# A one-layer diffusion block on one core: x first, modulation weights in larger groups, other feed order, five gate tiles in the scans

## The chip, the core and the metric

The kernel runs on one core of a Trainium2 chip. The metric is the device time of one execution in microseconds (us). A core has TensorE (PE in the profile; PEld is its weight load), VectorE (DVE), ScalarE (ACT), GpSimd (POOL), and SyncE (SP), which here issues all transfers. Each engine works through its own instructions in order. Which engine gets an instruction, and in what order, is settled when the program is built.

## The reference

One adaLN-modulated layer with two parallel head groups, cut to what matters here:

```python
mod = silu(c) @ w_ada + b_ada;  shift, scale, gate = split(mod, 3)     # w_ada: 2048 x 6144
h  = rms_norm(x, norm_w) * (1 + scale) + shift                         # x: 512 x 2048, latent tokens
hc = rms_norm(ctx, norm_w) * (1 + scale_c) + shift_c                   # ctx: 256 x 2048, with c_ctx
qkv_g, z_g, gates, q_a, k_a, v_a, z_a = split(h @ w_in)                # the same for hc
# group A, 8 heads of 128: q, k, v = silu(conv5(qkv_g)); chunked gated delta rule in 64-token chunks,
# forward and backward, context first, then latent; o = rms_norm(o_f + o_b) * silu(z_g)
# group B, 8 query heads on 2 kv heads: rms-normed q and k, rotary; softmax(q k / sqrt(128)) v * silu(z_a)
y = concat(A, B) @ w_out;   out = rms_norm(x + gate * y, final_norm_w)
```

All of it is float32. A product that needs full precision on fast matmuls is made of three: each operand is split into a rounded part (`hi`) and the rest (`lo`), and hi·hi, hi·lo and lo·hi are summed.

## The kernel before, in words

All projections are tiles of 128 output columns, accumulated over 16 K tiles (`KT`, 128 rows of the 2048 each), with three matmuls per K tile for the 512 latent tokens and, where it is needed, three for the 256 context tokens. A weight piece is four K tiles: a transfer, a cast to `hi` on ACT (L137), a subtraction that gives `lo` (L138; on DVE for the first 14 pieces, then on POOL).

**First stage.** Six blocks of 128 tokens (two of ctx, four of x) are loaded; ACT sums their squares (L284), POOL takes the power -0.5 (L224), DVE multiplies the block by 1/rms (L289), PE transposes it in 128x128 pieces (L295), and DVE and ACT copy the result to SBUF (L302, L300). For each group of K tiles (`GROUPS`, ten groups of one or two) `ada` reads the scale and shift columns of w_ada (32 MB in all, L315), multiplies them by the two conditioning vectors (L319) and turns the result into columns (L327). `make_h` forms h for a K tile on DVE (hf, L365), its hi on ACT (L367) and its lo on DVE (L373). `project` (L383, L385) then adds that K tile to five projections at once: k, q and v of head 0, k and q of head 1; the 32 gate columns (L388) follow at the end of each K tile. While a K tile is projected, `ada` of the group after the next one is slipped in between.

**From the first stage to the scans.** The five accumulators go to SBUF through `conv` (L199, L202: ACT copies from PSUM; L210 to L218: the convolution, its taps on DVE at L214). Gates, then `gdn_prep(0)`, prepare head 0. Meanwhile `feeding()`, a generator of projection matmuls, is drawn upon by `pull(n)` for n moving columns at a time: it is what PE does between the steps of other work.

**Scans.** For each head h, `gdn_scan` has 12 steps; each is a chain PE, DVE (rh, L818), PE (L827), ACT (L831, L834), PE (L838), DVE (state, L844). A step draws F1 + F2 + F3 = 9800 columns from the feeds, and `gdn_prep(h + 1)` runs in between. Before scan h starts, the loop pulls until v of head h + 1 has been fed. The feeds in order: v of head 1, the four tiles of attention's k and v, then for each head k, q, v and a tile of attention's q, and at the end `NZA` = 3 tiles of the attention gate z_a (`zal`), kept in DRAM.

**Attention.** 16 units (8 heads, two halves of 256 queries) and one for the last values. PE's order is written out by hand, and that of ACT, DVE and POOL too: transposed probabilities (L1218), scores (L154 to L156, `s`), `fill(FS)`, one more transpose, `fill(FV)`, values (`o`), `fill(FQ)`, on odd units the next head's q, `fill(FR)`. `fill(1)` is one K tile of the gate projections not made yet (`zl`, L1281: three matmuls of 512 columns): 13 tiles of 16 such fills, 12 fills a unit. Then the output projection (`po`) and the final norm.

## Time and profile before

Three runs took 1424.14, 1420.56 and 1421.66 us: the median is 1421.66 us. The profiled execution took 1418.51 us, its span on the core is 1416.3 us.

| engine | busy us | share of the span |
|---|---|---|
| PE | 1281.7 | 90% |
| PEld | 1021.2 | 72% |
| DVE | 767.8 | 54% |
| ACT | 614.5 | 43% |
| POOL | 517.3 | 37% |

In the views that follow, a row of a timeline has the start in us, the length in us, the engine, line, operation, output<-input with its shape, and in brackets how long the engine had been idle and what ended that. A row of the table by stage has for each engine its busy time and count of instructions, then the TensorE clock that was granted as a share of full speed (PEclk), the transfers' share of the 16 DMA engines, and GB/s. A wait is told as its total, the number of times, and the longest.

### The profile page before, as it was taken

How to read it: one execution, taken by the hardware profiler on the slowest of the kernel's cores; microseconds unless marked ns; L12 is line 12 of the kernel's file. 1: busy time of each engine (PE TensorE's matmuls, PEld its weight loads, DVE VectorE, ACT ScalarE, POOL GpSimd, SP SyncE). 2: the span in 40 equal slices, each digit the busy share in tenths (PEclk: the TensorE clock that was granted, in tenths of full speed). 3: DMA queues.
4: the chain of work that ended last, by engine and by line, in shares of the span. 5: the costliest groups of instructions: out<-in, count | busy, mean ns of one | idle time of the engine just before them, and what ended most of it. 6: DMA issues, size and time to landing. Idle time of an engine off the chain costs nothing.

```text
span 1416.3 us, 24550 instructions
## 1 busy us (share of the span) xinstructions
PE 1281.7 (90%) x9214; PEld 1021.2 (72%) x9214; DVE 767.8 (54%) x1666; ACT 614.5 (43%) x1531; POOL 517.3 (37%) x465
## 2 busy tenths in 40 slices
PE   4789979999999999999999999769989899999997
PEld 3345667888877877778777777547777778777785
DVE  5435487255565665656476643436666675544322
ACT  5212253334545445454444534445666663433221
POOL 1111300234434444343443534324877672011320
PEclk8999999999999999999999999879999999999999
DMA  8999412332232323223232344323555442474312
GB/s 263 328 346 290 120 53 59 93 67 66 78 66 59 72 69 75 62 57 84 58 77 61 81 90 121 96 86 113 150 148 161 129 112 60 163 236 143 92 37 95
DMA packets 234617, 163.49 MB, mean 115 GB/s; under 512 B 62146, under 2 KB 206619, under 8 KB 233475
## 3 DMA queue, kind: packets, MB, share of 16 engines
q1 hardware_dynamic: 234499, 161.93, 40.6%
q8 instruction: 72, 1.18, 0.4%
q14 instruction: 46, 0.38, 0.1%
HBM read 148.33 MB, written 13.56 MB: 114 GB/s over the span
## 4 chain that ended last, share of the span: by engine, by line
PE 52%; DVE 19%; issue 9%; ACT 7%; DMA 6%; POOL 5%; SPq 1%; POOLq 0%; DVEq 0%; ACTq 0%
PE vl L172 5%; PE zl L1281 4%; PE kl L172 3%; PE vx L174 3%; DVE cacc_v L214 3%; PE kvl L172 3%; DMA wada<-in_w_ada 2%; DVE cacc_k L214 2%; PE po L155 2%; PE tsh L838 2%; PE po L156 2%; PE po L154 2%; DVE rh L818 2%; DVE tmh L694 2%; PE ql L172 2%
## 5 line engine op out<-in xcount | busy, mean ns | idle before, releaser
L230 POOL TENSOR_TENSOR sdh<-sth,egl 128x256 f32<-128x256 f32 x80 | 55.7, 696 | 176.5 <-DVE sth L844 70.6
L1323 POOL TENSOR_TENSOR gacc<-graw,gacc 128x512 f32<-128x512 f32 x60 | 89.9, 1498 | 48.9 <-ACT graw L1321 38.8
L138 POOL TENSOR_TENSOR wlo_z<-wraw_z,whi_z 128x512 fp32r<-128x512 f32 x52 | 70.6, 1360 | 55.9 <-ACT whi_z L137 55.9
L823 ACT ACTIVATE oqh<-ksh,egsw 64x128 f32<-64x128 f32 x128 | 46.4, 362 | 100.4 <-DVE rh L818 99.5
L818 DVE SCALAR_TENSOR_TENSOR rh<-ksh,negeg,vtokh 64x128 f32<-64x128 f32 x176 | 61.1, 347 | 47.3 <-PE ksh L806 44.3
L1281 PE MATMUL zl<-hhL,whi_z 128*128 128x512 f32 x208 | 85.4, 411 | 0.0
L1281 PE MATMUL zl<-hL,whi_z 128*128 128x512 f32 x208 | 82.4, 396 | 0.0
L1281 PE MATMUL zl<-hhL,wlo_z 128*128 128x512 f32 x208 | 82.3, 395 | 0.0
L844 DVE TENSOR_TENSOR sth<-sdh,tsh 128x256 f32<-128x256 f32 x80 | 33.7, 421 | 89.5 <-PE tsh L838 84.3
L155 PE MATMUL po<-wlo_wo,mh 128*128 128x512 f32 x192 | 76.7, 399 | 3.8 <-DVE wlo_wo L138 3.8
L154 PE MATMUL po<-whi_wo,mh 128*128 128x512 f32 x192 | 76.0, 398 | 2.5 <-ACT whi_wo L137 1.5
L156 PE MATMUL po<-whi_wo,ml 128*128 128x512 f32 x192 | 76.0, 396 | 0.0
L138 DVE TENSOR_TENSOR wlo_wo<-wraw_wo,whi_wo 128x512 fp32r<-128x512 f32 x48 | 37.7, 794 | 64.7 <-ACT whi_wo L137 64.5
L838 PE MATMUL tsh<-vsh,ktok 128*128 128x128 f32 x352 | 58.0, 289 | 10.1 <-ACT vsh L831 5.3
L353 POOL TENSOR_TENSOR w0l<-w0r,w0h 128x640 fp32r<-128x640 f32 x16 | 24.9, 1561 | 107.4 <-PE cctx L388 56.4
L903 DVE TENSOR_TENSOR ptl<-pt,pth 128x512 fp32r<-128x512 f32 x48 | 31.9, 688 | 58.4 <-ACT pth L902 58.1
L1429 POOL TENSOR_TENSOR yx<-yx,tt 128x512 f32<-128x512 f32 x12 | 17.1, 1441 | 127.0 <-DVE tt L230 67.9
L838 PEld LDWEIGHTS tsh<-vsh,ktok 128*128 128x128 f32 x352 | 49.0, 196 | 18.7 <-ACT vnh L834 8.8
L214 DVE SCALAR_TENSOR_TENSOR cacc_v<-craw,cvT,cacc_v 128x256 f32<-128x256 f32 (+1 forms) x64 | 41.6, 696 | 33.9 <-ACT cacc_v L210 33.5
L827 PE MATMUL tsh<-rh,UU 128*128 128x128 f32 x176 | 38.4, 301 | 21.8 <-DVE rh L818 21.7
L137 ACT CAST whi_wo<-wraw_wo 128x512 fp32r<-128x512 f32 x48 | 29.3, 618 | 59.5 <-PE po L156 42.6
L827 PEld LDWEIGHTS tsh<-rh,UU 128*128 128x128 f32 x176 | 28.4, 194 | 33.7 <-issue 15.2
(492 smaller groups left out, 4155.4 us busy)
## 6 DMA issues: line engine op xcount, KB each, us to landing
wada<-in_w_ada SPq DMA_DIRECT2D x64, 512.0 KB, 8.0
graw<-in_w_ada SPq DMA_DIRECT2D x64, 256.0 KB, 2.7
wraw_z<-in_w_in SPq DMA_DIRECT2D x52, 256.0 KB, 3.0
wraw_wo<-in_w_out SPq DMA_DIRECT2D x48, 256.0 KB, 3.0
wraw_v<-in_w_in SPq DMA_DIRECT2D x28, 256.0 KB, 2.8
wraw_k<-in_w_in SPq DMA_DIRECT2D x24, 256.0 KB, 2.8
wraw_q<-in_w_in SPq DMA_DIRECT2D x24, 256.0 KB, 3.0
xs<-in_x SPq DMA_DIRECT2D x4, 1024.0 KB, 4.8
```

The lines of the kernel that those rows point to most:

```text
L138: (lo_eng or G).tensor_tensor(out=lo, in0=raw, in1=hi, op=ALU.subtract)
L154: T.matmul(out, lhsT=lh, rhs=rh, start=start, stop=False, skip_group_check=True)
L155: T.matmul(out, lhsT=lh, rhs=rl, start=False, stop=False, skip_group_check=True)
L156: T.matmul(out, lhsT=ll, rhs=rh, start=False, stop=stop, skip_group_check=True)
L172: T.matmul(pl, lhsT=lw, rhs=rt[0], start=st, stop=sp, skip_group_check=True)
L214: V.scalar_tensor_tensor(out=x, in0=raw[:, i0 + j:i0 + j + m], scalar=w(j), in1=x, op0=ALU.mult, op1=ALU.add)
L230: eng.tensor_tensor(out=out, in0=x, in1=y, op=ALU.mult)
L818: V.scalar_tensor_tensor(out=r[rows], in0=ks[rows, d], scalar=gsc["negeg"][rows, gcol:gcol + 1], in1=vtok[rows, p], op0=ALU.mult, op1=ALU.add)
L827: T.matmul(ts[:, 2], lhsT=UU[:, w], rhs=r, start=True, stop=True, skip_group_check=True)
L838: T.matmul(ts[:, d], lhsT=ktok[:, p, half], rhs=vs, start=True, stop=True, skip_group_check=True)
L1281: T.matmul(pl, lhsT=lw, rhs=rt, start=k == 0 and m == 0, stop=k == KT - 1 and m == 2, skip_group_check=True)
L1323: G.tensor_tensor(out=acc, in0=raw, in1=acc, op=ALU.add)
```

## The change

- **x first.** The transfers of x and ctx are issued ahead of the six small ones, and seven buffers of 1 MB instead of five (`BIG`) serve x and w_ada. DVE no longer multiplies a block of x: it makes a 128x128 diagonal matrix `rd` of 1/rms, and PE multiplies the block by it with an ordinary float32 matmul where there was a transpose. Six of eight copies out are DVE's.
- **Groups.** `GROUPS` = (2, 4, 4, 4, 2). `ada` handles shift and scale one after the other, with 1 MB transfers whose rows are 1 KB (two K tiles) or 2 KB (four). The gate columns become `gate_sums`, which stand right behind `make_h` of a pair of K tiles and ahead of that group's projections. Weights of K tile k + 2 are asked for when K tile k starts.
- **Accumulators.** `take` copies all five out of PSUM at once, ahead of the convolutions, two of them into new buffers (`xraw`). In the first piece of a feed with context tokens, the latent matmuls all come first.
- **Feeds.** New order; all `lo` pieces of feeds are POOL's. `NZA` is 5: two gate projections (2 x 48 matmuls of 512 columns) go from attention's fills to the feeds. FV is 3 (was 4), FR 2 (was 3): 10 fills a unit.

```diff
-FS, FV, FQ, FR = 4, 4, 1, 3
+FS, FV, FQ, FR = 4, 3, 1, 2
-NZA = 3
+NZA = 5
-    GROUPS = (1, 1, 2, 2, 2, 2, 2, 2, 1, 1)
+    GROUPS = (2, 4, 4, 4, 2)
...
-        if lo_eng is None and cnt[0] <= 14:
-            lo_eng = V
...
+            if pc is not None and kq == 0:
+                for out, m, n_ in ((pl, 0, SEQ), (pc, 1, CTX)):
+                    for x in passes:
+                        one(out, m, *x)
+                        yield n_
+                continue
...
+    def take(pl, pc, raw=None):
+        raw = next_craw() if raw is None else raw
         if pc is not None:
             S.copy(raw[:, 2:2 + CTX], pc)
+        S.copy(raw[:, CTX + 4:CTX + 4 + SEQ], pl)
+        return raw
...
-    BIG = 5
+    BIG = 7
...
-        V.tensor_scalar(out=xt_, in0=xt_, scalar1=ssx[:, t:t + 1], scalar2=None, op0=ALU.mult)
+        rd = p0.tile([128, 128], F32, tag="rd", bufs=2, name=f"rd{t}")
+        V.tensor_scalar(out=rd, in0=ident, scalar1=ssx[:, t:t + 1], scalar2=None, op0=ALU.mult)
...
+                T.matmul(tp[:, i], lhsT=xt_[:, c0:c0 + 128], rhs=rd, start=True, stop=True, skip_group_check=True)
...
-                T.transpose(out=tp[:, i], in_=xt_[:, c0:c0 + 128], identity=ident)
...
+        cols, rows = n * 128, 16 // n
+        for s in range(2):
+            ada_ps = gtile([128, 512], f"ada{g}_{s}")[:, :cols]
+            for j in range(KT // rows):
+                wt = big([128, rows, cols], f"wada{g}_{s}_{j}")
...
+    def gate_sums(p_):
+        for k in (2 * p_, 2 * p_ + 1):
+            for j in range(3):
+                T.matmul(gps[32 * j:32 * j + 32], lhsT=wg[:, k], rhs=hfs[k][:, 256 * j:256 * j + 256],
+                         start=False, stop=k == KT - 1, skip_group_check=True)
...
+    def ahead():
+        gate_sums(0)
+        yield
+        for g in range(1, len(GROUPS)):
+            yield from ada(g)
+            for p_ in make_h(g):
+                yield
+                gate_sums(p_)
+            made.add(g)
+            yield
...
+    todo = ahead()
     for g in range(len(GROUPS)):
+        while g not in made:
+            next(todo)
+        for k in range(first_k[g], first_k[g] + GROUPS[g]):
+            if k + 2 < KT:
+                first_weights(k + 2)
+            for i, _ in enumerate(project(k)):
+                if k or i >= 2:
+                    next(todo, None)
...
+    raws = [take(klat, cctx[:, 0]), take(qlat, None), take(vlat, cctx[:, 1]),
+            take(klat1, cctx1[:, 0], xraw[0]), take(qlat1, None, xraw[1])]
...
     def feeding():
+        yield from feed_kva(0)
+        yield from feed_qa(0)
+        yield from feed_kva(1)
         yield from feed_v(1)
-        for i in range(4):
-            yield from feed_kva(i)
-        fed.add("kva")
         for h in range(2, NH):
             yield from feed_k(h)
             yield from feed_q(h)
             yield from feed_v(h)
-            yield from feed_qa(h - 2)
-        for h in range(6, NH):
+            if h in (3, 5):
+                yield from feed_qa(1) if h == 3 else feed_kva(2)
+        yield from feed_kva(3)
+        fed.add("kva")
+        for h in range(2, NH):
             yield from feed_qa(h)
         for h in range(NZA):
             yield from feed_za(h)
```

**PE in the first stage, where a group's h is ready.** Names end in a buffer number; hf2 is h of K tile 2, klat0 the k of head 0, cctx1 holds the gate sums. Before, the gates of K tile 2 follow its projections:

```order
L319 MATMUL ada4_737<-wada4_2_764,cs_113 32x512 x4
L383 MATMUL qlat0_514<-hhL_70,w0h2_604 128x512
L383 MATMUL qlat0_514<-hL2_627,w0h2_604 128x512
L383 MATMUL qlat0_514<-hhL_70,w0l2_605 128x512
L319 MATMUL ada4_737<-wada4_3_774,cs_113 32x512 x4
L383 MATMUL qlat1_516<-hhL_70,w0h2_604 128x512
L383 MATMUL qlat1_516<-hL2_627,w0h2_604 128x512
L383 MATMUL qlat1_516<-hhL_70,w0l2_605 128x512
L388 MATMUL cctx1_518<-hf2_617,wg_428 32x256 x3
L383 MATMUL klat0_512<-hhL_70,w0h3_611 128x512
```

Now the second half of a group's modulation, then the gates of its four K tiles, and only then K tile 2's first projection:

```order
L333 MATMUL ada1_1_602<-wada1_1_0_603,cs_107 32x512 x4
L333 MATMUL ada1_1_602<-wada1_1_1_609,cs_107 32x512 x4
L333 MATMUL ada1_1_602<-wada1_1_2_615,cs_107 32x512 x4
L333 MATMUL ada1_1_602<-wada1_1_3_621,cs_107 32x512 x4
L341 MATMUL adat1_1_629<-cmain_75,part1_1_627 128x128 x4
L387 MATMUL cctx1_488<-hf2_637,wg_382 32x256 x3
L387 MATMUL cctx1_488<-hf3_642,wg_382 32x256 x3
L387 MATMUL cctx1_488<-hf4_659,wg_382 32x256 x3
L387 MATMUL cctx1_488<-hf5_664,wg_382 32x256 x3
L398 MATMUL klat0_482<-hhL_70,whi_w0_2_491 128x512
```

The gates moved from behind the projections of their own K tile to ahead of those of the whole group.

**ACT at the end of the first stage.** Before, the fourth accumulator (klat1) is copied only after the convolution of the first (cacc_k0) is done:

```order
L199 COPY craw1_1526<-cctx0_517 128x256
L202 COPY craw1_1526<-klat0_512 128x512
L202 COPY craw2_1527<-qlat0_514 128x512
L199 COPY craw0_1525<-cctx0_517 128x256
L210 ACTIVATE cacc_k0_1574<-craw1_1526,cvT_78 128x770
L202 COPY craw0_1525<-vlat0_513 128x512
L440 ACTIVATE adt_1509<-adt_1509 128x16
L470 ACTIVATE beta_83<-gx_1508 128x96
L475 ACTIVATE ug_1516<-ug_1516 128x96
L137 CAST whi_v1_3_1797<-wraw_v1_3_1795 128x512
L218 ACTIVATE craw1_1526<-cacc_k0_1574 128x512
```

Now all eight copies stand together:

```order
L200 COPY craw1_1509<-cctx0_487 128x256
L201 COPY craw1_1509<-klat0_482 128x512
L201 COPY craw2_1510<-qlat0_484 128x512
L200 COPY craw0_1508<-cctx0_487 128x256
L201 COPY craw0_1508<-vlat0_483 128x512
L200 COPY xraw0_1483<-cctx1_488 128x256
L201 COPY xraw0_1483<-klat1_485 128x512
L201 COPY xraw1_1484<-qlat1_486 128x512
L497 ACTIVATE beta_83<-gx_1491 128x96
```

Nothing of the convolutions is ahead of them any more.

**PE in the last scan.** Before, the feeds end in step 3 of 12 (tsh7_4 is step 4), and what follows is scan and the transposes that prepare attention:

```order
L172 MATMUL zal2a_9418<-hhL_70,wlo_z2a_3_9548 128x512
L804 MATMUL ksh7_9362<-sth7_3_9575,kq7_7952 128x128
L806 MATMUL ksh7_9362<-sth7_3_9575,kq7_7952 128x128
L907 MATMUL ktp00_9592<-cmain_75,ktok0_1652 128x128 x2
L827 MATMUL tsh7_4_9597<-rh7_4_9583,UU1_2182 128x128
L838 MATMUL tsh7_4_9597<-vsh7_4_9599,ktok1_1653 128x128 x2
```

Now step 8 still has feeds around it:

```order
L165 MATMUL zal1a_9532<-hhL_70,whi_z1a_3_9643 128x512
L165 MATMUL zal1a_9532<-hL6_1110,whi_z1a_3_9643 128x512
L865 MATMUL tsh7_8_9632<-vsh7_8_9634,ktok1_1643 128x128 x2
L874 MATMUL oh7_9341<-vnh7_8_9636,IB1_1651 128x128
L165 MATMUL zal1a_9532<-hhL_70,wlo_z1a_3_9644 128x512
L165 MATMUL zal1a_9532<-hhL_70,whi_z1a_3_9643 128x512
```

The feeds now last to the end of the scans: 67 matmuls of 512 columns stand behind the last head's output transposes (L892).

More of the change, by code (lines that the diff above doesn't have):

```diff
@@ L87, in build @@
     hhL = hp.tile([128, KT, SEQ], F32R, name="hhL")
-    GROUPS = (1, 1, 2, 2, 2, 2, 2, 2, 1, 1)
+    GROUPS = (2, 4, 4, 4, 2)
     first_k = [sum(GROUPS[:g]) for g in range(len(GROUPS))]
-    place = [(g, i) for g, n in enumerate(GROUPS) for i in range(n)]
     es_hc = ExitStack()
@@ L210, in conv @@
         S.activation(acc, raw[:, 0:n], AF.Copy, scale=w(0))
-        for i0, m in ((off, SEQ), (0, CTX))[:1 if pc is None else 2]:
+        for i0, m in ((off, SEQ), (0, CTX))[:2 if ctx else 1]:
             for j in range(1, 5):
@@ L215, in conv @@
                                        op0=ALU.mult, op1=ALU.add)
-        if pc is not None:
+        if ctx:
             S.activation(e[:, :CTX], acc[:, :CTX], AF.Tanh)
@@ L322, in ada @@
-        part = p0.tile([128, 512], F32, tag="part", bufs=2, name=f"part{g}")
-        V.tensor_copy(part[:, :2 * cols], ada_ps[:, :2 * cols])
-        yield
-        tp = gtile([128, 2 * n, 128], f"adat{g}")
-        for i in range(2 * n):
-            T.transpose(out=tp[:, i], in_=part[:, i * 128:(i + 1) * 128], identity=ident)
-        md = p0.tile([128, 2, 2, 2], F32, tag="md", bufs=4, name=f"md{g}")[:, :, :n]
-        V.tensor_reduce(out=md.rearrange("p s i m -> p (s i) m"),
-                        in_=tp.rearrange("p a (g m) -> p a m g", g=4)[:, :, 0:2], axis=AX.X, op=ALU.add)
@@ L354, in first_weights @@
-        w0[k] = hi, lo
+        src = rows[:, 0:2048].rearrange("p (s c) -> p s c", s=2)[:, :, 0:256]
+        hi, lo = wpiece(src, f"w0_{k}", 256)
+        raw, vhi, vlo = [p0.tile([128, 128], t_, tag=i, bufs=3, name=f"{i}{k}")
+                         for i, t_ in (("w0r", F32), ("w0h", F32R), ("w0l", F32R))]
+        SY.dma_start(raw, rows[:, COL_V:COL_V + 128])
+        S.copy(vhi, raw)
+        G.tensor_tensor(out=vlo, in0=raw, in1=vhi, op=ALU.subtract)
+        w0[k] = (hi[:, 0], vhi, hi[:, 1]), (lo[:, 0], vlo, lo[:, 1])
@@ L356, in build @@
     hfs = {}
     def make_h(g):
-        md = mds[g]
-        for i in range(GROUPS[g]):
-            k = first_k[g] + i
-            hf = hfs[k] = p0.tile([128, NTOK], F32, tag="hf", bufs=3, name=f"hf{k}")
-            for m_, t0, t1 in ((0, CTX, NTOK), (1, 0, CTX)):
-                V.tensor_scalar(out=hf[:, t0:t1], in0=xts[m_, g][:, i], scalar1=md[:, 1, i, m_:m_ + 1],
-                                scalar2=md[:, 0, i, m_:m_ + 1], op0=ALU.mult, op1=ALU.add)
-                S.copy(hh[m_][:, k], hf[:, t0:t1])
@@ L409, in build @@
     gps = cctx1[:, 1]
+    todo = ahead()
     for g in range(len(GROUPS)):
-        if g + 1 < len(GROUPS):
-            group_h(g + 1)
-        ahead = ada(g + 2) if g + 2 < len(GROUPS) else iter(())
-        for i in range(GROUPS[g]):
-            for _ in project(first_k[g] + i):
-                next(ahead, None)
-        for _ in ahead:
-            pass
+        while g not in made:
[6 more added lines that the diff above has]
+                    next(todo, None)
     es0.close()
@@ L430, in build @@
     SY.dma_start(ctri, a["ctri"])
+    es_x = ExitStack()
+    px_ = es_x.enter_context(tc.tile_pool(name="px", bufs=1, side="right", reuse_waits="tile"))
+    xraw = [px_.tile([128, 774], F32, name=f"xraw{i}") for i in range(2)]
     es1a = ExitStack()
@@ L526, in build @@
     craw = [cvp.tile([128, 774], F32, name=f"craw{i}") for i in range(3)]
-    for t in craw:
+    for t in craw + xraw:
         for i in (0, CTX + 2, NTOK + 4):
```

190 lines of the change are left out of this document (95 added, 95 removed).

## Prediction

> **What bounds the kernel now.** I began with the table by stage. Its stretches end where PE's first modulation, first projection, last waits for w_ada, last accumulated K tile, first scan, last feed and first attention unit stand. A row has the stretch, its length, busy us and instructions of PE, PEld, DVE, ACT and POOL, the granted clock, the transfers' share and GB/s; five units of attention follow.
>
> ```profile
> 38.10:48.30 10.20, 5.69 (x70) 2.56 (x69) 3.52 (x12) 2.62 (x6) 2.64 (x2) 0.82 1.08 303
> 48.30:89.50 41.20, 33.07 (x197) 15.19 (x195) 12.05 (x29) 6.43 (x12) 5.07 (x4) 0.96 1.10 347
> 89.50:180.10 90.60, 90.50 (x573) 56.76 (x570) 43.36 (x78) 21.29 (x41) 22.44 (x25) 1.00 0.77 228
> 180.10:272.50 92.40, 79.79 (x720) 67.49 (x721) 61.94 (x189) 34.50 (x91) 12.35 (x12) 0.94 0.27 65
> 272.50:896.70 624.20, 589.77 (x5309) 490.74 (x5309) 358.91 (x890) 290.59 (x818) 261.77 (x254) 1.00 0.30 74
> 896.70:945.10 48.40, 26.16 (x126) 20.51 (x125) 19.26 (x44) 20.16 (x69) 11.71 (x14) 0.69 0.15 49
> 945.10:1192.00 246.90, 230.49 (x1230) 188.13 (x1231) 161.28 (x242) 146.57 (x312) 156.59 (x113) 0.98 0.47 133
> ...
> 977.40:991.80 14.40, 14.40 (x85) 12.35 (x83) 8.75 (x16) 8.97 (x20) 7.27 (x5) 1.00 0.32 95
> 991.80:1010.00 18.20, 15.60 (x86) 12.38 (x84) 13.92 (x19) 11.76 (x25) 15.76 (x13) 1.00 0.56 159
> 1010.00:1024.60 14.60, 14.60 (x86) 12.42 (x84) 8.67 (x14) 9.06 (x22) 10.52 (x8) 1.00 0.50 138
> 1024.60:1045.10 20.50, 16.38 (x87) 12.46 (x85) 14.28 (x21) 12.53 (x25) 16.30 (x13) 1.00 0.55 165
> ```
>
> PE sets the time nearly everywhere. So a change is worth what it takes from PE's idle time, from PE's work, or from time at a low clock. The first projection starts at 48.3. To 89.5 PE waits 8.1 us for transfers; from there to 180.1 it is idle for 0.1. The end of the last scan is the worst stretch: 22.2 of 48.4 us idle, clock 0.69. Even units of attention are all PE; odd ones are idle for 2.6 and 4.1.
>
> Next the waits of PE, for the stretches 180.1 to 272.5 and then 272.5 to 896.7 (total, times, longest).
>
> ```profile
> PE kvx L174 <- ACT craw L199: 6.0, 1, 6.0
> PE tvh L707 <- DVE grh L230: 2.3, 1, 2.3
> ```
>
> ```profile
> PE tsh L827 <- DVE rh L818: 14.9, 18, 1.8
> ```
>
> **The change part by part.** The sum is made against the profiled execution: span 1416.3, its own time 1418.5, which is 3.1 below the median of the runs.
>
> (a) *x first.* From the timeline:
>
> ```profile
> 1.18 0.42 SPq L237 DMA_DIRECT2D vrow<-in_c  x1
> ...
> 3.77 0.87 SPq L273 DMA_DIRECT2D xs<-in_ctx  x2
> ...
> 9.04 1.16 ACT junk L284 x2
> ...
> 11.90 0.57 POOL ssx L224
> ...
> 13.83 3.25 PE L295 MATMUL xt<-cmain,xs 128*128 128x128 f32 x14 [8.27 <-DVE xs L289]
> ...
> 35.02 3.12 PE L295 MATMUL xt<-cmain,xs 128*128 128x128 f32 x22 [0.49 <-DVE xL L302]
> 38.07 1.93 PE L319 MATMUL ada<-wada,cs 128*32 128x256 f32 x32
> ...
> 860.75 0.60 PE L838 MATMUL tsh<-vsh,ktok 128*128 128x128 f32 x4
> 861.19 0.39 PE L847 MATMUL oh<-vnh,IB 128*128 128x128 f32 x2
> ```
>
> The first block's transfer is issued at 1.2 instead of 3.8. PE begins at 13.8 now, thus at 11.2 by the earlier issue; the diagonal (128x128) takes the place of a pass over 128x2048 on DVE, which is worth about another 1.1. I take 10.1. Two ordinary float32 matmuls of 128x128 on L838 (a matmul leaves two records) take 0.44 us from their start to the next line's, or 0.22 each; 22 transposes in a row took 3.12, or 0.14. So the 96 pieces cost 96 x 0.22 = 21.1 us where transposes would cost 13.6. Today they stretch over 24.2 us, since PE waits for x and for copies, much of it at half clock. With 1.1 for a cold start PE is done at 32.3. The modulation vectors, now behind x, are no longer hidden: 2.2 for their matmul and copy, 34.5. `ada(0)` costs two rounds of matmuls (1.9 now for one half of the work, so about 2.0 each), copy, transposes and reduction, 0.95 a half, and 0.9 for the sums: 41.3. Then 2.0 to the first h: 43.3 instead of 48.3, **-5**. Bounds: -9 (no cold start, vectors hidden) to +20, which is the matmuls at double price.
>
> By the Trainium skill, "TensorE: Matmul & The Clock Gate", section Terms, trn2's matmul has a transpose mode that is 4 times faster for FP32, which speaks against this edit. The rows above show 0.22 against 0.14, a ratio of 1.6. With 4 x 0.14 a piece costs 0.57, and the sum of all parts would come out about 34 higher.
>
> (b) *Groups and the gate sums in the rest of stage 1.* Larger groups mean fewer, longer transfers. What they add stands on PE: the second half of a group's modulation, then the gate sums, wait for DVE's h, and the projections wait behind them in PE's queue. DVE's steps:
>
> ```profile
> 41.03 0.18 DVE L329 TENSOR_REDUCE md<-adat 128x4 f32<-128x16 f32 x1 [0.53 <-PE adat L327]
> ...
> 41.70 0.55 DVE L365 TENSOR_SCALAR hf<-xL,md 128x512 f32<-128x512 f32 x1
> 42.17 0.41 DVE L365 TENSOR_SCALAR hf<-xC,md 128x256 f32<-128x256 f32 x1
> 42.94 0.69 DVE L373 TENSOR_TENSOR hL<-hf,hhL 128x512 fp32r<-128x512 f32 x1 [0.36 <-ACT hhL L367]
> 43.55 0.42 DVE L373 TENSOR_TENSOR hC<-hf,hhC 128x256 fp32r<-128x256 f32 x1
> ```
>
> ```profile
> L365 DVE TENSOR_SCALAR hf<-xL,md x16: 543/1872/1882, 41.7 to 164.1; 128x512 f32<-128x512 f32 x16
> ```
>
> Sums of modulation take about 0.63, hf of two K tiles 1.75 by the pitch of these rows, their lo 2.0, hf of the second pair 1.75: 6.1. Group 1 has nothing between but its own gates (two K tiles, 1.1), so PE waits 5.0. In groups 2 and 3 two projections come in between: 2.5 each. Group 4 has one pair: 0.6. That is 10.6. The second row (shortest, median, longest, in ns) shows that most hf take 1.87 instead of 0.54: POOL's lo of the weights runs at these times. All 14 contended would add 14 x 1.33 = 18.6; POOL's work here starts with each K tile, so I take a third, 6.2. Total 16.8 of waits. It replaces the 8.2 that PE is idle from 48.3 to 180.1 and 1.3 lost to the clock (0.04 of 33.1): **+7.4**. Bounds: +1.2 with no contention, +20 with all of it. Transfers aren't late in this sum: the 20.8 MB up to group 1's last piece (6.3 of x and ctx, 12.6 of w_ada for six K tiles, the rest weights) are in by about 60 at the 347 GB/s of the second row, and PE wants them at 62.
>
> The contention has a rule too. In the Trainium skill, "GPSIMD Engine Reference", section "1. Specifications", GpSimd shares its SBUF interfaces with VectorE, with contention for DVE instructions in a 2-port mode or with two SBUF inputs. The row's 543 against 1872 ns agrees; taken as always in force it gives this term's upper end, and 1414 for the whole.
>
> (c) *Accumulators, and feeds at the start.* The waits of 6.0 (for the copy of the fourth accumulator, behind a convolution on ACT) and 2.3 go; of the clock's loss (0.06 of 79.8, 4.8) I take 1: **-9**. Bounds -2 (another wait of the same convolutions takes their place: DVE is 61.9 of 92.4 busy, and `take` makes nothing on it faster) to -13.
>
> (d) *Scans.* With two more tiles at the end of the feeds, and attention's k, v and q spread otherwise, a head's convolutions come within 98K columns of fed work instead of 123K, a quarter denser. The wait for rh, 14.9, is DVE's: a quarter more is **+3.7**. Bounds -4 (the same columns spread better) to +12.
>
> (e) *The last scan.* Idle 22.2, and the clock's 0.31 of 26.2 is 8.1: 30.3 in all. Now feeds stand in every step. In the scans before PE idled for 34.4 us in 84 steps, 0.4 a step; over eight steps 3.2 remains: **-27**. The two gate tiles' own 96 matmuls do not appear here: they go into idle time, or into the time in which other feeds ran earlier; their PE time is the same in both places. Bounds -17 (clock stays low for a third of it) to -30.
>
> (f) *Attention.* 32 fills, a K tile each of three 512-column matmuls, leave it. Their pitch:
>
> ```profile
> 896.09 0.39 PE L172 MATMUL zal2a<-hL,whi_z2a 128*128 128x512 f32 x1
> 896.32 0.40 PE L172 MATMUL zal2a<-hhL,wlo_z2a 128*128 128x512 f32 x1
> ```
>
> 0.234 x 3 x 2 = 1.40 us of PE a unit, 22.5 in 16 units. This work moves to the feeds, where (e) has found room for it: against the old total, attention must shorten by 22.5 to keep PE's balance. Even units, all PE, do. The odd ones are idle already and have a chain of softmax on ACT, DVE and POOL (15.8 of 18.2 us busy on POOL): the seven that bring the next head's q, if they do not shorten, give 7 x 1.4, **+10** of new idle. Bounds 0 to +22.5.
>
> How (e) and (f) fit: the sum counts idle time and lost clock only, since PE's total work stays, but for the 7.5 of (a), which its times contain.
>
> Sum: -5 + 7.4 - 9 + 3.7 - 27 + 10 = -19.9. The span comes to 1396.4, the profiled execution to 1398.6, the median to **1402**.
>
> **The rivals.**
>
> *R1: attention follows its fills in full.* Term (f) is 0, thus 1392. For it: POOL, the fullest of the others in odd units, has fewer lo pieces of gate weights to make there too. Against it: PE is idle for 2.6 and 4.1 in the odd units shown, so PE's work isn't what ends them.
>
> *R2, the other side: the diagonal matmuls on the path.* From x's landing to the first projection everything waits for these 96. They decide at 0.22 + 19.9/96 = 0.43 us each, which is half clock throughout: 1421. At 0.57 it is 1436. For it: PE waits often there, and the clock falls when it does (transposes of x14 in 3.25 at 13.83, twice the price of those at 35.02). Against it: PE will wait less than now.
>
> *R3, the other side too: the scan's chain behind the taps.* DVE's long instructions are now denser beside rh:
>
> ```profile
> L214 DVE SCALAR_TENSOR_TENSOR cacc_v<-craw,cvT,cacc_v 128x256 f32<-128x256 f32 (+1 forms) x64 | 41.6, 696 | 33.9 <-ACT cacc_v L210 33.5
> ```
>
> If each of 96 steps met half a tap more, 0.35, that is +33.6 in place of +3.7: 1432. It decides at 0.24 a step. Against it: 14.9 of waiting in 18 places now, and PE has feeds to run meanwhile.
>
> *R4: x first and the groups don't do what they say.* Rows of 1 or 2 KB move no faster, and group 1's 8 MB are late by 6 us: 1408. The stretch to 89.5 has its DMA engines full at 347 GB/s, which speaks for it. Against it: that rate is today's, with rows of 0.5 and 1 KB, and no row shows what limits it.
>
> **How the numbers follow.** 0.3% of the median, 4.3 us, is about what a measurement of this kernel can tell from no change: faster is below 1417.4, slower above 1425.9. Chances: the forecast 0.58 (0.53 of it faster, 0.04 same, 0.01 slower), R1 0.22 (faster), R2 0.07 (0.02 same, 0.05 slower), R3 0.05 (slower), R4 0.08 (0.06 faster, 0.02 same). Faster 0.81, same 0.08, slower 0.11. The forecast's own range is 1390 to 1416: the bounds of (b), (c) and (f) as independent of each other give 12 down and 19 up, and I cut the latter to 14, since each upper bound needs its whole effect in every group or unit. To hold 8 in 10 it takes in R1 and the half clock of R2: 1384 to 1420.
>
> **What would show it.** (a) the first projection at 43, and pieces of L295's successor at 0.22 with full clock; at 48 or later R2 or the vectors' chain is right. (b) PE's waits for hf ahead of the gate sums of 5, 2.5, 2.5 and 0.6 plus some contention, the end of stage 1 at about 182; more than 16 of them means contention, waits for wada mean R4. (c) No wait for the fourth accumulator's copy; a new one of over 5 there undoes it. (d) Waits for rh below 20 in the scans; over 30 is R3. (e) The last scan dense, clock 1.00. (f) Even units 13.0, odd ones 17 to 20; odd ones shorter by 1.4 are R1. Wrong is the forecast outside 1390 to 1416, and wrong in its main step if the last scan still leaves more than 10 us idle.

## The result, and the profile after

The changed kernel takes 1431.16 us (median of 4 runs, 1429.25 to 1432.45) against 1421.11 us of the kernel before: a ratio of 1.0066, with a 95% interval of 1.0047 to 1.0085. It is slower by 0.7%, where 1402 us were forecast. The profiled execution has a span of 1427.5 us, 11.2 more than before. One execution of experiment 12 below took 3129 us, more than twice its other three, and is left out there.

The table by stage, first of the kernel before, then of the changed one. The stretches end at the same events in both: first projection, end of the first stage, first rh of the first scan, first rh of the last scan, last transposes of its output, first transposed probabilities, last ones, end. Columns as in the prediction.

```profile
0.00:48.30 48.30, 25.13 (x167) 17.43 (x167) 23.48 (x65) 25.47 (x60) 6.76 (x15) 0.86 0.87 271
48.30:180.10 131.80, 123.57 (x766) 71.95 (x764) 55.42 (x107) 27.71 (x52) 27.50 (x29) 0.99 0.87 265
180.10:277.60 97.50, 84.30 (x747) 71.36 (x748) 63.99 (x193) 36.00 (x94) 14.68 (x14) 0.95 0.27 64
277.60:876.60 599.00, 567.82 (x5195) 473.49 (x5195) 348.22 (x867) 280.49 (x788) 249.13 (x241) 1.00 0.30 74
876.60:945.90 69.30, 44.40 (x216) 34.41 (x214) 27.90 (x63) 29.55 (x99) 22.01 (x24) 0.78 0.20 63
945.90:959.50 13.60, 13.58 (x57) 10.87 (x57) 4.93 (x9) 6.68 (x17) 4.37 (x3) 0.88 0.74 247
959.50:1205.70 246.20, 228.79 (x1242) 187.35 (x1241) 162.78 (x244) 144.66 (x304) 156.07 (x113) 0.99 0.44 123
```

```profile
0.00:43.80 43.80, 29.14 (x262) 26.65 (x262) 20.48 (x71) 21.00 (x44) 8.76 (x18) 1.00 0.95 329
43.80:180.30 136.50, 126.53 (x764) 75.51 (x764) 39.30 (x95) 27.68 (x63) 30.50 (x46) 0.94 0.72 244
180.30:286.80 106.50, 88.71 (x733) 73.88 (x733) 71.32 (x182) 40.48 (x108) 38.52 (x30) 0.89 0.28 67
286.80:861.10 574.30, 533.55 (x5061) 449.88 (x5060) 335.62 (x861) 268.92 (x761) 228.46 (x227) 0.99 0.28 68
861.10:948.90 87.80, 78.81 (x397) 64.45 (x396) 30.77 (x67) 40.15 (x118) 40.85 (x40) 0.94 0.33 89
948.90:975.80 26.90, 26.89 (x122) 21.54 (x121) 3.70 (x8) 8.54 (x16) 11.57 (x9) 1.00 0.82 258
975.80:1217.40 241.60, 212.61 (x1150) 173.01 (x1149) 163.78 (x248) 141.05 (x300) 147.51 (x105) 0.98 0.42 118
```

Rows (a) to (c) compare lengths. Work has moved between the later stretches, so (d) to (f) are compared by what PE loses there: length less busy time (idle), and busy time multiplied by the missing part of the clock. Against the terms of the forecast (us):

| term of the forecast | forecast | measured | from |
|---|---|---|---|
| (a) to the first projection | -5 | -4.5 | 48.3, 43.8 |
| (b) projections | +7.4 | +4.7 | 131.8, 136.5 |
| (c) to the first rh | -9 | +9.0 | 97.5, 106.5 |
| (d) heads 0 to 6, idle and lost clock | +3.7 | +15 | 31.2 idle; 40.8 idle and 1% of 533.6 |
| (e) last scan and after it | -27 | -22.6 | 24.9 idle, 11.4 clock; 9.0 idle, 4.7 clock |
| (f) attention, idle and lost clock | +10 | +13.6 | 17.4 and 2.3; 29.0 and 4.3 |

The measured column adds up to 15.2 where the spans differ by 11.2; busy times are modelled at their ends, and the clock is rounded to a hundredth, which in (d) alone can be worth 3 us. By rows, (c) misses by 18 us and (d) by 11. By parts of the change, runs 1, 4 and 6 below show something that the rows hide: what makes the kernel slower than before is the move of the two gate tiles out of attention.

**Where (c) went.** PE's waits from 180.3 to 286.8 in the changed kernel:

```profile
PE tsh L854 <- DVE UU L800: 6.5, 1, 6.5
PE gtp L488 <- DVE gso L486: 3.4, 2, 2.1
PE qal0a L165 <- POOL wlo_q0a L131: 3.4, 1, 3.4
PE tvh L734 <- DVE grh L237: 3.0, 1, 3.0
```

The wait for the copy of an accumulator (6.0 before) is gone, as forecast. The one for grh is not: it has grown from 2.3 to 3.0. New are 3.4 us for a `lo` piece that is now GpSimd's, and 6.5 us for UU (0.9 before). VectorE shows what stands ahead of UU:

```profile
273.43 0.35 DVE L800 COPY UU<-pxyh 32x192 f32<-32x192 f32 x1 [2.96 <-PE pxyh L793]
273.79 5.54 DVE L221 SCALAR_TENSOR_TENSOR cacc_v<-craw,cvT,cacc_v 128x512 f32<-128x512 f32 x8
279.36 0.74 DVE L800 COPY UU<-pxyh 32x192 f32<-32x192 f32 x2
```

UU is four short copies, the last step of head 0's preparation, and the first scan cannot begin without them. Between the first and the second stand the eight taps of head 1's v, 5.5 us in one piece. v of head 1 used to be the first feed; it is now the fourth, and its convolution comes due at this very place. PE stops for 6.5 us. The clock granted in the whole stretch is 0.89, where it was 0.95.

**Where (d) went.** PE's wait for rh in heads 0 to 6, before:

```profile
PE tsh L827 <- DVE rh L818: 13.9, 17, 1.8
```

In the changed kernel, with two waits that the kernel before does not have; DTh and grh belong to the preparation of the next head:

```profile
PE tsh L854 <- DVE rh L845: 12.8, 11, 1.8
PE pxyh L782 <- DVE DTh L764: 6.1, 2, 4.0
PE tvh L734 <- DVE grh L237: 3.9, 2, 1.9
```

The wait of 4.0 us for DTh, a transposition on VectorE, is in head 4. From VectorE's timeline:

```profile
678.42 2.20 DVE L221 SCALAR_TENSOR_TENSOR cacc_v<-craw,cvT,cacc_v 128x512 f32<-128x512 f32 x4
680.53 0.58 DVE L763 COPY_PREDICATED DDh<-cmain,pxbh 128x384 f32<-128x384 uint32 x1
681.01 1.15 DVE L234 SCALAR_TENSOR_TENSOR vv<-craw,cacc_v 128x256 f32<-128x256 f32 x4
682.07 0.57 DVE L764 STREAM_TRANSPOSE DTh<-DDh 128x384 f32<-128x384 f32 x1
```

Again taps stand ahead of a step of a preparation. Before, a scan drew 122,880 columns and the feeds had exactly as many for a head (k, q, v and a tile of attention's q), so a convolution met each scan at the same place. Now most heads have 98,304 columns, while a scan draws about 113,700 by the program's order (the first of its 12 steps draws no F1): the convolutions drift through the scans and sooner or later meet the places where they do harm. PE's idle time head by head bears this out. Before it was 3.2, 5.1, four times 4.7, and 4.1 us; in the changed kernel it is 5.4, 6.1, 5.2, 3.7, 8.0, 7.1 and 5.3.

### The profile page after: what moved, and what is told of

It is laid out like the page before. It is cut to its first block, busy times and chain, and to the rows that moved or that the text cites. A ratio compares the mean times of both kernels' runs of the same rounds, so it can differ in the third digit from the quotient of the medians.

```text
span 1427.5 us, 24690 instructions
## 1 busy us (share of the span) xinstructions
PE 1290.5 (90%) x9310; PEld 1038.8 (73%) x9310; DVE 745.3 (52%) x1645; ACT 611.3 (43%) x1527; POOL 543.0 (38%) x501
## 5 line engine op out<-in xcount | busy, mean ns | idle before, releaser
L131 POOL TENSOR_TENSOR wlo_z<-wraw_z,whi_z 128x512 fp32r<-128x512 f32 x44 | 62.4, 1422 | 62.9 <-ACT whi_z L130 62.9
L1314 PE MATMUL zl<-hhL,whi_z 128*128 128x512 f32 x176 | 73.4, 417 | 0.0
L1314 PE MATMUL zl<-hL,whi_z 128*128 128x512 f32 x176 | 70.4, 400 | 0.0
L1314 PE MATMUL zl<-hhL,wlo_z 128*128 128x512 f32 x176 | 69.9, 397 | 0.0
L131 POOL TENSOR_TENSOR wlo_v<-wraw_v,whi_v 128x512 fp32r<-128x512 f32 x28 | 38.0, 1359 | 56.1 <-ACT whi_v L130 55.9
L1354 ACT ACTIVATE graw<-graw,scol 128x512 f32<-128x512 f32 x60 | 43.1, 725 | 23.9 <-DMA graw<-in_w_ada 22.2
L131 POOL TENSOR_TENSOR wlo_k<-wraw_k,whi_k 128x512 fp32r<-128x512 f32 x24 | 30.8, 1283 | 56.6 <-ACT whi_k L130 54.0
## 6 DMA issues: line engine op xcount, KB each, us to landing
wada<-in_w_ada SPq DMA_DIRECT2D x32, 1024.0 KB, 11.5
xs<-in_x SPq DMA_DIRECT2D x4, 1024.0 KB, 11.1
```

Of the source, the lines that this page charges most:

```text
L131: (lo_eng or G).tensor_tensor(out=lo, in0=raw, in1=hi, op=ALU.subtract)
L1314: T.matmul(pl, lhsT=lw, rhs=rt, start=k == 0 and m == 0, stop=k == KT - 1 and m == 2, skip_group_check=True)
L1354: S.activation(acc if k == 0 else raw, raw, AF.Copy, scale=scol[:, k:k + 1])
```

## The experiments

Each run has its own measurements of the kernel before (medians 1419.8 to 1422.3). All runs change the new kernel, unless said otherwise.

**1. Fills as before.**

```diff
-FS, FV, FQ, FR = 4, 3, 1, 2
+FS, FV, FQ, FR = 4, 4, 1, 3
-NZA = 5
+NZA = 3
```

> The changed kernel with the fills and the number of gate tiles in the feeds as before (12 fills a unit, NZA 3). Theory: attention pays for its lost fills with new idle time, about 18 us of the 22.5; so attention (first transposed probabilities to last) takes 245 to 249 us instead of 241.6, the 18.6 us of dense feeds after the last scan go, and the time is 1413 to 1419. Rival (the idle time in attention comes from something else, such as the early gates on VectorE): attention takes 264, and the time stays at 1428 to 1434.

1416.26 us, ratio to before 0.9969 (0.9955 to 0.9982). Attention has 246.4 us instead of 241.6, and the dense feeds behind the last scan (67 matmuls of gate tiles, with no idle time between them) are gone. 22.5 us of work had left attention and made it 4.8 shorter: the theory holds. The same work had made the way from the first rh of the last scan to attention 17.2 us longer (97.5 here, 114.7 in the changed kernel).

**2. lo parts on VectorE.**

```diff
     def split(raw, nm, lo_eng=None):
+        if not nm.startswith("w0"):
+            cnt[0] += 1
+            if lo_eng is None and cnt[0] <= 14:
+                lo_eng = V
```

> The changed kernel with the lo parts of the first 14 weight pieces of the feeds on VectorE, as before, instead of GpSimd. Theory: GpSimd's work slows VectorE between the first stage and the scans (the copies gso of 32x256 take 1.1 to 1.6 us instead of 0.27), so the stretch from 180.3 to the first rh shrinks from 106.5 by 5 to 9 and the time is 1422 to 1427. Rival (the order of the convolutions and of v of head 1 decides, and the lo parts only load VectorE more): no gain, 1430 to 1434.

1433.81 us, ratio 1.0097 (1.0080 to 1.0114). The stretch to the first rh has 107.1 us, no shorter. PE's wait for gso falls from 3.4 to 0.9, but a wait of 11.5 for wlo_q0a appears, now on VectorE, and the one for UU stays at 6.5. The rival's time is met: what VectorE gains at gso it loses by having the `lo` parts to make.

**3. v of head 1 first.**

```diff
+        yield from feed_v(1)
         yield from feed_kva(0)
         yield from feed_qa(0)
         yield from feed_kva(1)
-        yield from feed_v(1)
```

> The changed kernel with v of head 1 as the first feed again, ahead of attention's k, q and k; all else as changed. Theory: VectorE has v1's convolution right before the first scan, and UU waits behind it (PE waits 6.5 us); with v1 early that wait goes, the first rh comes 5 to 8 us earlier and the time is 1423 to 1427. Rival (VectorE has the same convolutions ahead of the scan anyway, only earlier, where they delay head 0's preparation): the wait gets another name, 1429 to 1434.

1426.73 us, ratio 1.0034 (1.0012 to 1.0055). The wait for UU is 0.9, the stretch to the first rh 99.3. Runs 5 and 7, with the same order, have it at 102.2 and 102.1 (one profile each), and run 1, with the changed order, at 106.8. So the order of the feeds cost 4 to 7 of the 18 us. The runs scatter widely (1418 to 1430). A wait of 5.3 for grh is left.

**4. The kernel before with the new fills.** Lines as in run 1, the other way round.

> The kernel before with only the fills and gate tiles changed (10 fills a unit, NZA 5). Theory: the 22.5 us of work fit into the idle time at the end of the last scan, and attention shortens by 4 to 6 only: 1414 to 1419. Rival (attention follows its fills in full where nothing else is changed): attention 224, the time 1396 to 1402.

1423.97 us, ratio 1.0017 (1.0000 to 1.0034). Attention is 238.9 instead of 246.2: of 22.5 us it gives back 7.3. The last scan takes 10 us more. Neither number was met, but the rival is far off. Moving the tiles gains nothing in the kernel before either.

**5. Runs 1 and 3 together.**

> The changed kernel with fills and NZA as before and v of head 1 as the first feed. Theory: the two losses are independent (attention 15, transition 7), so the time is 1406 to 1412, with the first rh at 276 to 279 and attention at 245 to 248. Rival (convolutions in the scans shift by the earlier start and take the gain back): heads 0 to 6 get over 5 us longer in all, 1413 to 1418.

1413.02 us, ratio 0.9923 (0.9894 to 0.9952), just above the theory's 1412 and at the lower end of the rival's. Heads 0 to 6 have about the same length as in run 1 (578 and 577), so the rival's loss of 5 us there is not seen.

**6. Fills and the whole order of the feeds as before.** The body of `feeding` is the old one; first stage, `take` and GpSimd's lo parts stay new.

> The changed kernel with fills, NZA and the whole order of the feeds as before; first stage, accumulators' copies and lo parts on GpSimd stay changed. Theory: what the scans lost is the phase of the convolutions: with 122880 columns a head again each scan has them at the same place, idle time and lost clock of heads 0 to 6 come to 30 to 37 us (changed kernel 47, before 33), the last scan loses 33 to 37 again, and the time is 1415 to 1421. Rival (the lo parts on GpSimd or the accumulators' copies slow the scans): heads 0 to 6 stay above 43, the time 1424 or more.

1418.11 us, ratio 0.9966 (0.9949 to 0.9983). Heads 0 to 6, then the last scan:

```profile
277.20:875.00 597.80, 565.47 (x5195) 471.44 (x5194) 347.43 (x866) 279.96 (x788) 247.68 (x241) 1.00 0.30 74
875.00:943.60 68.60, 43.88 (x216) 33.92 (x214) 27.92 (x63) 29.43 (x99) 22.05 (x24) 0.80 0.20 64
```

32.3 us idle in the heads at full clock (before 31.2, changed 40.8), and the last scan loses its 34 again. The theory holds: it is the new order that adds idle time to the scans, and not GpSimd or `take`. It also fills the last scan, and in the time the two cancel: 0.9966 here and 0.9969 in run 1, which differ in nothing but the order. Run 1 and the changed kernel (1.0066) differ in nothing but the two tiles and the fills.

**7. Run 5, with later gate sums in the first stage.** For a group's last pair of K tiles they stand four projections later:

```diff
-            for p_ in make_h(g):
+            hs, np_ = make_h(g), GROUPS[g] // 2
+            for i in range(np_):
+                p_ = next(hs)
                 yield
-                gate_sums(p_)
+                if i + 1 < np_:
+                    gate_sums(p_)
+            next(hs, None)
             made.add(g)
+            for _ in range(4):
+                yield
+            gate_sums(p_)
             yield
```

> As the run with fills as before and v1 first, and in the first stage the gate sums of a group's last pair of K tiles stand four projections later, so that PE does not wait for that pair's h. Theory: waits for hf (8.2) fall to 3 to 5 and less clock is lost (7.6), so the stretch from the first projection to the end of the first stage takes 129 to 133 instead of 136 and the time is 1402 to 1408. Rival (the projections wait for the same h, or the clock is lost to what comes next): 135 to 137, the time as without it.

1399.87 us, ratio 0.9847 (0.9823 to 0.9871): 13 us below run 5, more than expected. The projections take 125.3 us instead of 133.6 to 136.5:

```profile
42.70:168.00 125.30, 121.85 (x764) 74.59 (x764) 42.17 (x95) 27.05 (x63) 28.91 (x46) 0.97 0.78 269
```

Waits of PE for hf, first in the changed kernel, then here:

```profile
PE cctx L387 <- DVE hf L373: 8.2, 5, 2.2
```

```profile
PE cctx L387 <- DVE hf L373: 2.1, 2, 1.6
```

The gate sums cost 6 us of waiting, and clock that goes with it (0.94 of 126.5 in the changed kernel, 0.97 of 121.9 now: 7.6 and 3.7 lost). Against run 5 the stretch is 8.3 us shorter; the rest of the 13 us is not all accounted for.

**8. Transposes instead of the diagonal matmul**, with x multiplied by 1/rms on VectorE as before, x still first.

```diff
-        V.tensor_scalar(out=rd, in0=ident, scalar1=ssx[:, t:t + 1], scalar2=None, op0=ALU.mult)
+        V.tensor_scalar(out=xt_, in0=xt_, scalar1=ssx[:, t:t + 1], scalar2=None, op0=ALU.mult)
...
-                T.matmul(tp[:, i], lhsT=xt_[:, c0:c0 + 128], rhs=rd, start=True, stop=True, skip_group_check=True)
+                T.transpose(out=tp[:, i], in_=xt_[:, c0:c0 + 128], identity=ident)
```

> The changed kernel with x multiplied by 1/rms on VectorE and transposed as before, x first as changed. Theory (a piece costs 0.14 instead of 0.25 us on PE, VectorE has 1.3 us more a block and then sets the pace at about 3.3 us a block): first projection at 40 to 42 instead of 43.8, the time 1428 to 1431. Rival (the pass over x on VectorE holds everything up, as before): first projection at 45 to 47, the time 1433 to 1436.

1435.46 us of two runs, ratio 1.0093 (1.0064 to 1.0122); the first projection is at 44.7 us, between the two expectations. PE's first rows, of the changed kernel and of this one:

```profile
10.02 24.20 PE L301 MATMUL xt<-rd,xs 128*128 128x128 f32 x192 [10.02 <-DVE rd L295]
```

```profile
11.02 5.54 PE L300 MATMUL xt<-cmain,xs 128*128 128x128 f32 x32 [11.02 <-DVE xs L294]
19.79 5.48 PE L300 MATMUL xt<-cmain,xs 128*128 128x128 f32 x32 [3.22 <-DVE ssx L290]
28.28 6.58 PE L300 MATMUL xt<-cmain,xs 128*128 128x128 f32 x32 [3.01 <-DVE xs L294]
```

On average a diagonal piece takes 24.2 / 96 = 0.25 us and a transpose of the quickest row 5.48 / 32 = 0.17, but PE then waits for VectorE between blocks. The runs that share the changed kernel's start have the first projection at 42.7 to 45.2 us, so 44.7 is no clear difference: the dearer instruction costs nothing here.

**9. Run 7, with the six small memsets of the new buffers on VectorE.** In the changed kernel GpSimd's large memsets stand behind them and fall together with VectorE's copies gso:

```profile
179.95 2.84 POOL L1024 MEMSET ktok<- 128x1536 f32 x2
182.73 2.13 POOL L1030 MEMSET IB<- 128x1024 f32 x2
```

```profile
181.39 1.53 DVE L485 COPY gso<-gsb 32x256 f32<-32x256 f32 x1
182.85 1.11 DVE L486 COPY gso<-gsb 32x256 f32<-32x256 f32 x1
```

> As the run with the gate sums later (1400 us), and the six small memsets of the two new buffers stand on VectorE, so that GpSimd's large memsets (ktok, IB, 5 us) no longer queue behind them until the first stage has ended. Theory: these memsets slow VectorE's copies gso from 0.27 to 1.1 to 1.6 us each, PE waits 3.4 us for them and then has half clock; without that the stretch to the first rh takes 95 to 99 instead of 102 and the time is 1393 to 1397. Rival (the convolutions behind the copies end at the same time anyway): 101 to 103 and no gain.

1399.68 us, ratio 0.9859 (0.9835 to 0.9883): no gain in the times. The stretch is 98.8 us instead of 102.1 in one profile each, and the wait for gso is 2.2 instead of 3.4. The change did only part of what it was for: the large memsets start earlier, at 167.0 us, but last to 171.8 and still run beside the copies, which take 0.8 to 1.1 us. What the memsets cost in all stays open.

**10. Run 9, with head 1's k and q convolved behind head 0's preparation.** `gdn_post_k(1, ...)` and `gdn_post_q(1, ...)` stand ahead of `run(g1, ...)` instead of right behind `gdn_post_v(0, ...)`.

> As the run with the memsets moved, and the convolutions of head 1's k and q stand on VectorE behind the preparation of head 0, not ahead of it; v of head 1 is still the first feed and its taps still come ahead of grh. Theory: grh is late because of taps ahead of it, 8 of 20 remain, so PE's wait of 5.3 us for grh falls to 1 to 4 and the time is 1 to 4 us below that of the run with the memsets moved. Rival (the moved taps delay UU or DTh instead): a new wait of over 3 us there, no gain.

1395.17 us, ratio 0.9822 (0.9796 to 0.9848), 4.5 below run 9. The wait for grh falls from 5.3 to 1.2, but one for DTh grows from 1.7 to 4.0: the theory's gain and the rival's wait both came. `take` had let these convolutions run earlier, which put them ahead of head 0's grh.

**11. Run 10, with v of head 1 as the second feed.**

> As the run with head 1's convolutions later, and v of head 1 is the second feed, so that no taps of head 1 but three stand ahead of grh. Theory: no wait for grh over 1 us and no half clock after it; the stretch to the first rh takes 91 to 95, the time is 4 to 8 us below that of the run with the memsets moved. Rival (the later taps come ahead of UU, as they do in the changed kernel): a wait of 3 to 7 for UU, no gain against it.

1400.47 us, ratio 0.9857 (0.9839 to 0.9876): no gain against run 9, and slower than run 10. No wait of over 1 us for UU or grh is left, but 4.3 us go to another copy of the gates (gts) and 2.5 to egl. The stretch has 97.9 us. VectorE is busy for 64 to 71 of these 95 to 107 us in the versions before, changed, 3 and 14; a better order moves the wait, and each one removed uncovers some of the next.

**12, 13. Run 10 with one gate tile more in the feeds (NZA 4), and one fill fewer a unit**, at its end (FR 2) or ahead of the values (FV 3).

> As the run with head 1's convolutions later (1395 us), with one gate tile more in the feeds (NZA 4) and one fill fewer at the end of each unit (FR 2); 11.2 us of PE work leave attention. Theory: these fills cover the wait of the next unit's transposes for VectorE's qTl (8.4 us in the changed kernel, 4.6 before); attention takes 242 to 245 instead of 245.9, and the time is 1396 to 1401. Rival (only the fills before the values matter): attention 235 to 238, the time 1390 to 1394.

> The same with the fill taken from before the values instead (NZA 4, FV 3, FR 3). Theory: these fills cover the wait of the values for ptl and pth (7.7 us in the changed kernel, 4.0 before) and are paid for alike: attention 241 to 245, the time 1396 to 1401. Rival (only the fills at the end of a unit matter): attention 235 to 238, the time 1390 to 1394.

1405.34 us (median of three), ratio 0.9900 (0.9876 to 0.9924), and 1408.38 us, 0.9928 (0.9901 to 0.9955). Attention has 250.0 and 255.0 us, more than the 245.9 of run 10 with more work. Neither expectation was high enough.

**14. Run 10 with the convolutions held in phase.**

```diff
-    F1, F2, F3 = 3900, 2700, 3200
+    F1, F2, F3 = 3260, 2257, 2675
...
-            if h in (3, 5):
-                yield from feed_qa(1) if h == 3 else feed_kva(2)
+        yield from feed_kva(2)
         yield from feed_kva(3)
         fed.add("kva")
-        for h in range(2, NH):
+        for h in range(1, NH):
             yield from feed_qa(h)
```

> As the run with head 1's convolutions later, with 8192 columns a step instead of 9800 (F1, F2, F3 = 3260, 2257, 2675) and no other tile between the heads' k, q and v in the feeds: each scan then draws exactly the 98304 columns of one head. Theory (the phase of the convolutions is what the new order cost in the scans): idle time and lost clock of heads 0 to 6 fall from 48 to 25 to 38, these heads take 530 to 550 instead of 577, the last scan is filled, 40 to 55 us of dense feeds follow it, and the time is 1370 to 1386. Rival (with fewer columns a step the chain of a step bounds PE): heads keep 0.5 us or more of idle time a step, 45 us or more in all, 1388 to 1397.

1372.47 us, ratio 0.9667 (0.9648 to 0.9685): 3.3% below the kernel before. Heads 0 to 6, the last scan, and the dense feeds behind it:

```profile
263.60:766.70 503.10, 480.14 (x4840) 403.79 (x4839) 320.89 (x863) 256.17 (x742) 209.29 (x208) 1.00 0.28 67
766.70:849.00 82.30, 70.69 (x364) 57.83 (x363) 31.32 (x67) 36.12 (x112) 36.25 (x35) 0.95 0.29 79
849.00:914.40 65.40, 65.39 (x287) 52.51 (x286) 3.70 (x8) 19.22 (x35) 29.74 (x23) 1.00 0.59 171
```

The heads are idle for 23.0 us, less than in the kernel before, at full clock. The chain of a step does not bound PE with 8192 columns a step. The time is as the theory said; the heads are shorter than its 530 to 550, because I had counted only part of the columns that leave them. Head by head they are idle for 3.2, 2.4, four times 2.8, and 6.1 us: again about the same from scan to scan. The last scan is still idle for 11.6 us and loses some clock. That the phase, and not the smaller number of columns in a scan, makes the difference is argued: no run had the same columns in another phase, and the kernel before, in phase too, was idle for 4.7 a head.

**15. Run 14 with more fills** (NZA 2, FV 5: 13 fills a unit).

> The run with 8192 columns a step, and 11.2 us of gate projections moved from the dense feeds after the last scan into attention (NZA 2, FV 5, 13 fills a unit). Theory (attention has idle PE time that its fills pay back, about a third of what is moved): attention gets 5 to 9 longer, 11.2 leave the dense feeds, the time is 2 to 6 below that run. Rival (attention's units are PE-bound at 12 fills): attention 11 longer, no gain.

1382.20 us, ratio 0.9732 (0.9710 to 0.9753). The dense feeds lose 11.1 us, attention gains 18.9, more than the work that moved; neither expectation foresaw that. Fewer fills (runs 12 and 13) and more fills both lengthen it.

**16, 17. Run 14 with 12 fills a unit in other places**: 5, 3, 1, 3 and 5, 4, 1, 2 instead of 4, 4, 1, 3.

> The run with 8192 columns a step, 12 fills a unit as there, but one of them ahead of the last transposes instead of ahead of the values (FS 5, FV 3). Theory (the place counts: fills ahead of the values cover the wait for pth and ptl): attention 249 to 254 instead of 245.1, waits for pth and ptl 8 to 14 instead of 3, the time 1376 to 1382. Rival (the number of fills a unit counts, since gate tiles of 16 fills then begin at other places in the units): attention 244 to 247, the time 1371 to 1375.

> The same with the fill taken from the end of a unit (FS 5, FR 2). Theory (the place counts: fills at the end cover the wait of the next transposes for qTl): attention 248 to 253, waits of the transposes 12 or more instead of 6, the time 1375 to 1381. Rival (the number counts): attention 244 to 247, the time 1371 to 1375.

1383.72 us, ratio 0.9753 (0.9724 to 0.9781), and 1381.05 us, 0.9727 (0.9708 to 0.9746). Attention has 259.7 and 255.9 us instead of 245.1: moving one fill of 0.7 us costs 11 to 15 us in 16 units. PE's waits in attention, of run 14, then of run 16:

```profile
PE pt L1257 <- DVE qTl L937: 4.5, 5, 1.9
PE o L147 <- ACT pth L936: 1.7, 3, 1.0
PE o L148 <- DVE ptl L937: 1.4, 4, 0.3
PE pt L1257 <- ACT qn L1205: 0.6, 1, 0.6
```

```profile
PE o L147 <- ACT pth L936: 5.5, 4, 1.6
PE o L148 <- DVE ptl L937: 4.1, 8, 1.0
PE pt L1257 <- ACT qn L1205: 4.1, 5, 1.0
PE pt L1257 <- DVE qTl L937: 0.8, 3, 0.5
```

The place counts: the waits for pth and ptl grow by 6.5 and that for qn by 3.5, while that for qTl falls. Of run 16's 14.6 us more, idle time explains 5.4 (17.7 to 23.1) and lost clock 7 (0.97 of 236.6 busy); about 2 are open. In run 17 the transposes wait longer, as the theory said, but not for qTl (4.5 to 2.2): the wait for qn grows from 0.6 to 7.5. Both runs put the fill at the same new place, so what it costs there is not told apart from what it costs to take it away.

## Why the prediction was wrong, by its steps

**(a) was right in size.** The first projection came at 43.8 (43.3 forecast). The price of a piece was right: from 15.3 us on, 84 pieces take 18.9 us, 0.22 each. Ahead of that the first 12 take 5.3 us, 0.44 each, so R2's double price did come, for an eighth of the pieces. The cold start cost 2.6 us; the prediction had 1.1, for which it showed no row. PE's records, two a piece, in 4 us of each part:

```profile
11.00:15.00 4.00, 4.00 (x21) 4.00 (x20) 1.69 (x6) 2.77 (x7) 0.55 (x1) 1.00 1.01 428
17.00:21.00 4.00, 4.00 (x39) 4.00 (x38) 2.59 (x9) 3.97 (x10) 0.98 (x2) 1.00 1.01 325
```

PEclk reads 1.00 in both, but the trace has no record of the clock ahead of 15.3 us. So the 96 pieces took 24.2 us where 22.2 were forecast, and the modulation behind them 9.6 where it was 11.0. With 84 pieces at 0.22, and with transposes (run 8) no earlier, R2 falls. (Where R2 calls the transposes at 13.83 twice the price of those at 35.02, its rows give 0.23 and 0.14 us.) The Trainium skill's page "TensorE: Matmul & The Clock Gate", section Terms, has the transpose mode 4 times faster for FP32; at full clock the runs show 0.22 us for a piece and 0.11 for a transpose (run 8, from 24.1 to 24.6 us), twice, and the measurement decides.

**(b) was nearly right, by two errors that cancel.** The waits for hf were 8.2, not 16.8: VectorE's hf of x took 0.55 us in the median instead of 1.87, so the contention that I added (6.2) was not there. The row of the changed kernel:

```profile
L373 DVE TENSOR_SCALAR hf<-xL,md x16: 534/545/686, 42.6 to 151.1; 128x512 f32<-128x512 f32 x16
```

By the Trainium skill's page "GPSIMD Engine Reference", section "1. Specifications", the two engines share their SBUF interfaces, with contention for VectorE instructions in a 2-port mode or with two SBUF inputs. That is no contradiction: before, 11 of the 16 hf had a lo part of GpSimd beside them, now three, and these three took 0.68 us. The rule taken as always in force would have been 20 us in this term. The clock, which the sum left out, lost 7.6. Run 7 shows that the step was the place to mend: moved gate sums are worth 8 us of the stretch against run 5 (11 against the changed kernel) and 13 in the times.

**(c) is the step that failed most**, +9.0 for -9. It took both waits of 6.0 and 2.3 off in full. The first went; the second, for grh, grew to 3.0, and one of 6.5 for UU came. The bound "another wait of the same convolutions takes their place" was named, at -2, and then -9 was taken in spite of VectorE's 62 of 92 us; the result lies outside the bounds. What I did not work out is where on VectorE the convolutions would stand after the move. Runs 3, 5 and 7 show 4 to 7 us of the stretch for v of head 1, run 10 shows 4.5 us of the time for k and q of head 1. The sign that the prediction gave for this, a new wait of over 5 us there, is what the profile shows (UU, 6.5). Even run 14 has 94.6 us in this stretch, 2.9 below the kernel before: 6 of the 9 us that were forecast were found by no run.

**(d) was mis-sized**, +15 for +3.7 and a bound of +12. I scaled one wait, that for rh, by the density of the convolutions; it did not grow (13.9 before, 12.8 after). What came were waits of the next head's preparation (DTh and grh, 10.0 us in all), and the view above shows taps ahead of the longest. That they meet by phase, not by density, is what runs 6 and 14 and the idle time head by head speak for. R3 gave 1432 by a tap in front of each rh, and 1431 was measured; the number agrees by chance, since rh is not where it happened.

**(e) came out near its size, but for another reason**, -22.6 for -27: the last scan is filled, but idle for 9.0 and with 4.7 of lost clock, not 3.2. From the first rh of the last scan to the first transposed probabilities PE was idle for 24.9 us before, 18.3 with the two tiles alone (run 4), 13.1 with the new order alone (run 1) and 9.0 with both. The new order did more of it than the tiles: seven scans now draw fewer columns (113,700 for 122,880), and what they leave comes at the end.

**(f) was somewhat too small, and its premise failed**, +13.6 for +10. The prediction let 22.5 us of work leave attention because (e) "has found room for it". The new order had taken most of that room, and 67 of the tiles' 96 matmuls come behind the last scan, where there is no idle time to fill. Against run 1 the two tiles lengthen the way from that rh to attention by 17.2 us and shorten attention by 4.8, and they cost 14.9 us in the times (1416.26 to 1431.16). In the kernel before (run 4) that way grew by 9.7 and attention shrank by 7.3. So the same idle time was counted on for two kinds of work. The size of (f) was worked out from odd units that bring the next head's q. Runs 12 to 17 show more: fills cover waits at certain places, and units without them lengthen. R1 (attention follows in full) falls. So does R4: none of PE's waits from 43.8 to 180.3 us was for a transfer.

Sum of the misses: 18 + 11 + 4 + 4, less 3 in (b), makes 34 where 31 us lie between the forecast and the measured span. The forecast's range went by the bounds of (b), (c) and (f) alone, and left out those of (a), (d) and (e).

## What to carry to other kernels

A tile of filler work has a tail on another engine, here a convolution of 5.5 us on VectorE; when the order of the fillers changes, look up on that engine what short link of a chain the tail will stand in front of. Where a loop draws filler by a fixed amount, try the amount that equals the work of one round, so that the tails meet each round at the same place: with what it left over for the end of the loop this was worth 22.7 us (run 14 against run 10). Price fillers by the place that they cover, not by their sum. And where two parts of a change both count on the same idle time, count it once.
